# Raw columns for the first group's projections: the reciprocal root applied on the way out of PSUM

## The chip, the cores and the metric

The kernel runs on one core of a Trainium2 chip. Its time is the device time in microseconds of one execution; several executions are timed, and the median is the figure compared. TensorE (PE, with PEld for its weight loads) multiplies matrices into PSUM; VectorE (DVE), ScalarE (ACT) and GpSimd (POOL) work on tiles of 128 partitions; the SyncE queue (SP) issues nearly all transfers, and GpSimd those that add while they write.

## The reference

One layer of a streaming encoder, for 2048 tokens of width 1024, with 16 heads of 64, in float32:

```python
def rms_norm(x, g):
    y = xf * lax.rsqrt(jnp.mean(xf * xf, axis=-1, keepdims=True) + RMS_EPS)
    return (y * g).astype(x.dtype)
...
h = rms_norm(x, g_pre_mix)
m = chunk_relpos_attention(h, w_qkv, w_o, rel_bias)   # 64-token chunks; own chunk and 8 before
x = x + rms_norm(m, g_post_mix)
h = rms_norm(x, g_pre_ffn)
x = x + rms_norm(swiglu(h, w_gate, w_up, w_down), g_post_ffn)
```

The factor of `rms_norm` is one number per token. So the query, key or value of a token can be projected from `x * g` and multiplied by the token's reciprocal root afterwards: both orders give the same result up to rounding.

## The kernel before

Tokens lie in columns: x is held as eight tiles ("columns" k = 0 to 7 in the code) of 128 features by 512 tokens for each half s of a group. There are two groups of 1024 tokens, each with two halves. Every float32 operand is split into a rounded part `hi` and the rest `lo`, and each product is three matmuls (`products`, lines 188 to 190): hi x hi, lo x hi, hi x lo. A query or key block of a head pair p and a half (`qk_job`) is two times eight k-steps of such a triple, 48 matmuls of 512 columns; the values of two head pairs (`v_job`) are 96 matmuls of 256 columns.

TensorE's order is written by hand: a loop over 64 slots per group places scores, transposes and outputs of the attention, and `fill` lets the generator `dense` yield projection matmuls in between, at a rate worked out from when each block is due. All other engines follow an order that a scheduler makes from the program. Small jobs that go with the projections wait in the queue `later`; `tick` takes them from there, one credit for each triple of 512 columns, and `drain` empties it at once. Transposes of scores, the reload of weights and the weight sums for the feed-forward part (`weight_sums`, copies on the SP queue and adding transfers on GpSimd) run alongside.

`begin` is the prologue of group 0. It loads the weights of the first query and key pair (plan[0]) and the eight columns of the first half, splits the columns after multiplying by the gain only (lines 1152 and 1153), and runs query and key projections of the first pair over them, one after the other; the squares are added by GpSimd (line 240). `rstd_steps` sums them over features by matmuls with a vector of ones (`pssq`, line 254), takes the power on GpSimd (line 258) and spreads the root over partitions by four transposes (`prs`, line 270). The first half's queries, keys and values are multiplied by the root when they leave PSUM (lines 1198 and 1203). The second half is loaded into `prep`, squared, and normalised (line 317) and split (lines 340 and 341) before its projections run. Afterwards the first half is loaded once more (`again`), normalised and split, so that all later projections of group 0 read normalised columns. `keep_qk` (lines 474 and 475) splits a query or key block out of PSUM into `stage`, from where transfers put it into `q` and `k`. `said.add(("start", g))` then lets the attention of group 0 begin.

The rows of the relative bias go through a tile `ext` to `ext_d` in memory, at the very start.

Of the kernel before, what the change touches and what calls it, by code (L numbers as in the profile page):

```python
# [47 lines left out]
def trunk(  # L48
# [32 lines left out]
    ones = const.tile([P, P], F32, name="ones")  # L81
# [334 lines left out]

    bias_bufs = []
# [17 lines left out]
    def v_job(g, s, j, w):  # L435
# [6 lines left out]
        for t2 in range(2):  # L442
# [25 lines left out]
    def keep_qk(g, s, p, which, t, scale=None):  # L468
# [3 lines left out]
        scale = (0.125, 1.0)[which] if scale is None else scale  # L472
# [354 lines left out]
    def down_at(c):  # L827
        here = slice(c, min(c + 2, NC))
        return {n: w_d[BLOCK_AT[n]][:, here, :] for n in BLOCK_AT}, {n: sum_d[n][:, here, :] for n in sum_d}

    units = [gate_up_at(c) for c in range(NC)] + [down_at(c) for c in range(0, NC, 2)]
# [299 lines left out]
    def begin(weights):  # L1131

        ap = phase["ap"]
        a, b = heads
        u = Cols(0)
        stage = hb_tile(2, F32, (KT, HALF))
        raw = hb_tile(3, F32, (KT * HALF,))
        for n in range(2):
            ready.append([w_tile(f"{n}_{c}") for c in range(2)])
        second = Prep(1, x[1], PRE_MIX)  # L1140
        second.buffer()
        g_ = gt[:, PRE_MIX, :]
        for k in range(KT):
            if k % 2 == 0:
                s = slice(k * 256, k * 256 + 512)
                sp.dma_start(raw[:, s], plan[0][:, s])
                to = ready[0][k // 4]
                part = slice(k % 4 * 256, k % 4 * 256 + 512)
                split_part(to[0][:, part], to[1][:, part], raw[:, s])
            h = stage[:, k, :]  # L1150
            sp.dma_start(h, x[0][:, k, :])
            act.activation(u.hi(k), h, AF.Copy, scale=g_[:, k : k + 1])
            dve.scalar_tensor_tensor(
                u.lo(k), h, g_[:, k : k + 1], u.hi(k).bitcast(F32), op0=ALU.mult, op1=ALU.subtract
            )
        total = xp.tile([P, HALF], F32, tag="io", name="total_0", bufs=3)
        for k in range(KT):
            add_square(stage[:, k, :], total, k == 0, pool)
        for c in range(2):
            s = slice(c * 1024, c * 1024 + 1024)  # L1160
            part = raw[:, 2048 + c * 1024 : 3072 + c * 1024]
            sp.dma_start(part, plan[1][:, s])
            split_part(*ready[1][c], part)
        for k in range(KT):
            sp.dma_start(second.t[:, k, :], x[1][:, k, :])
        qw = take(ahead=False)
        vw = take(ahead=False)
        rstd = nrm_tile("rstd_0")
        r = const.tile([P, 4], F32, name="rstd_col")
        pts = []  # L1170
        for which in range(2):
            pt = ps.tile([P, HALF], F32, tag="mm", name="pqk")
            c = slice(which * P, which * P + P)
            for k in range(KT):
                products(pt, qw.hi(k, c), qw.lo(k, c), u.hi(k), u.lo(k), k == 0, k == KT - 1)
                yield 3 * C512
            pts.append(pt)
# [3 lines left out]
        def square(k):  # L1181
            return 0.4, lambda: add_square(second.t[:, k, :], second.total, k == 0)

        later.extend(pause(1.5) + rstd_steps(total, rstd, 4.0, keep=r, bank=bank))
        later.extend([square(k) for k in range(KT)] + second.rstd(4.0, bank))
        both = zip(second.norm(), second.split(odd=pool))
        later.extend((0.2, step) for pair in both for _, step in pair)
        v = ap.tile([P, 4, 256], F32, tag="v", name="v_0", bufs=5)
        for t2 in range(2):
            pt = phase["psa"].tile([P, 2, 256], F32, tag="tt", name="pv_", bufs=2)  # L1190
            for n in range(2):
                c = slice((2 * t2 + n) * P, (2 * t2 + n) * P + P)
                for k in range(KT):
                    products(pt[:, n, :], u.hi(k, c), u.lo(k, c), vw.hi(k), vw.lo(k), k == 0, k == KT - 1)
                    yield 3 * C256
            for n in range(2):
                m = 2 * t2 + n
                act.activation(v[:, m, :], pt[:, n, :], AF.Copy, scale=r[:, m : m + 1])
        vs[0, 0, 0] = v
        ts = []  # L1200
        for which in range(2):
            t = xp.tile([P, HALF], F32, tag="io", name="t", bufs=3)
# [292 lines left out]
```

## Time and profile before

| | us |
|---|---|
| median of 3 runs | 2457.96 (2454.76 to 2458.51) |
| the profiled execution | 2454.59 |
| its span, first to last instruction | 2452.8 |
| TensorE busy | 2403.4 (98%) |
| VectorE busy | 1461.6 (60%) |
| ScalarE busy | 1030.7 (42%) |
| GpSimd busy | 295.4 (12%) |

The profile is one execution. Rows of instructions in order of time give the start, the length, engine, line, operation, what is written and read, and in square brackets the idle time ahead and what ended it. A matmul's length overlaps that of the next, so the pace of a run of matmuls is read from start to start. Rows of waits give the total in us, the number of times, and the longest. Rows of stretches give for each engine the busy time and the number of instructions, then the granted TensorE clock, the share of the transfer engines and GB/s. Columns of the second half appear as `prep`, the raw first half as `hb`, blocks on the way out as `stage`.

### The profile page before, as it was taken

The page shows a single profiled execution, that of the slowest core. Times are in us where ns is not written, and L with a number is a line of the kernel's source. Part 1 is how long each engine was busy: PE and PEld are TensorE (multiplying, and loading weights), DVE is VectorE, ACT ScalarE, POOL GpSimd, SP SyncE. Part 2 cuts the span into 40 slices and gives each one's busy share as a digit, 9 for nine tenths or more (in the row PEclk, how much of TensorE's full clock was granted, in tenths as well). Part 3 has the DMA queues.
Part 4 walks back from the last instruction along what each step waited for, and adds up shares of the span by engine and source line. Part 5 has one row for each costly group of instructions (what it writes and reads, how often), then busy time and mean ns, then how long its engine had stood idle before and what let it go on. Part 6 is the DMA issues. An engine that isn't in the chain of part 4 may idle for free.

```text
span 2452.8 us, 34801 instructions
## 1 busy us (share of the span) xinstructions
PE 2403.4 (98%) x12536; PEld 1990.3 (81%) x12536; DVE 1461.6 (60%) x2552; ACT 1030.7 (42%) x1801; POOL 295.4 (12%) x370
## 2 busy tenths in 40 slices
PE   7999999899999999999999999999999999999997
PEld 5887878678888888778888888888888888888886
DVE  6644454567555554558566665677666655555577
ACT  4433444553444443455433333355443333334444
POOL 3122222201222222210000000000000000000001
PEclk9999999999999999999999999999999999999999
DMA  6667897956887867547576755377667665457654
GB/s 186 193 177 194 239 248 199 280 193 207 220 214 199 237 166 196 126 142 238 174 227 212 250 170 188 100 249 252 210 218 256 213 191 154 134 171 244 191 189 149
DMA packets 205276, 490.51 MB, mean 200 GB/s; under 512 B 24848, under 2 KB 26912, under 8 KB 203824
## 3 DMA queue, kind: packets, MB, share of 16 engines
q1 hardware_dynamic: 195312, 453.68, 58.4%
q0 software_dynamic: 9792, 34.61, 8.6%
q8 instruction: 99, 1.62, 0.3%
q14 instruction: 73, 0.60, 0.1%
HBM read 358.64 MB, written 148.42 MB: 207 GB/s over the span
## 4 chain that ended last, share of the span: by engine, by line
PE 54%; DVE 1%; DMA 1%; issue 0%; ACT 0%; DVEq 0%; SPq 0%
PE pd L189 6%; PE pd L188 6%; PE pd L190 6%; PE pb L188 5%; PE pb L189 5%; PE pb L190 5%; PE pa L188 3%; PE pa L189 3%; PE pa L190 3%; PE pc L188 3%; PE pc L190 3%; PE pc L189 3%; PE mm L188 1%; PE mm L190 1%; PE mm L189 1%; DMA y<-y 0%
## 5 line engine op out<-in xcount | busy, mean ns | idle before, releaser
L547 ACT ACTIVATE sc<-sc,nmax 128x640 f32<-128x640 f32 (+4 forms) x256 | 193.1, 756 | 278.4 <-DVE nmax L543 277.8
L188 PE MATMUL mm<-hb,whi 128*128 128x512 f32 x720 | 296.9, 412 | 2.9 <-ACT hb L340 2.4
L189 PE MATMUL mm<-hb,whi 128*128 128x512 f32 x720 | 283.5, 394 | 1.6 <-DVE hb L341 1.0
L190 PE MATMUL mm<-hb,wlo 128*128 128x512 f32 x720 | 283.8, 394 | 0.0
L551 POOL TENSOR_SCALAR sc<-sc,rows 128x640 f32<-128x640 f32 (+4 forms) x256 | 189.6, 742 | 688.1 <-DVE rows L550 652.4
L543 DVE CUSTOM_DVE_ANT_0 sc<-st,bias 128x640 f32<-128x640 f32 (+4 forms) x256 | 179.5, 737 | 104.0 <-PE st L535 101.0
L188 PE MATMUL pb<-hb,whi_gu_T 128*128 128x512 f32 x528 | 206.0, 390 | 3.1 <-DVE terms L955 3.1
L190 PE MATMUL pb<-hb,wlo_gu_T 128*128 128x512 f32 x528 | 205.5, 389 | 0.0
L189 PE MATMUL pb<-hb,whi_gu_T 128*128 128x512 f32 x528 | 205.4, 389 | 0.0
L258 POOL TENSOR_TENSOR rs<-ms,neg_half 128x4 f32<-128x4 f32 (+1 forms) x12 | 17.7, 1479 | 1252.4 <-DVE ms L256 805.7
L188 PEld LDWEIGHTS mm<-hb,whi 128*128 128x128 f32 x720 | 136.1, 189 | 38.4 <-issue 14.6
L190 PEld LDWEIGHTS mm<-hb,wlo 128*128 128x128 f32 x720 | 135.7, 188 | 29.7
L189 PEld LDWEIGHTS mm<-hb,whi 128*128 128x128 f32 x720 | 136.2, 189 | 24.6 <-DVE hb L341 2.5
L188 PE MATMUL mm<-whi,hb 128*128 128x256 f32 x480 | 142.0, 296 | 1.0 <-DVE stage L475 1.0
L189 PE MATMUL pd<-a,whi_d_T 128*128 128x512 f32 (+1 forms) x368 | 140.0, 380 | 0.4 <-DVE a L341 0.4
L188 PE MATMUL pd<-a,whi_d_T 128*128 128x512 f32 (+1 forms) x368 | 140.0, 380 | 0.0
L190 PE MATMUL pd<-a,wlo_d_T 128*128 128x512 f32 (+1 forms) x368 | 139.7, 380 | 0.0
L188 PE MATMUL pa<-hb,whi_gu_B 128*128 128x512 f32 x352 | 137.5, 391 | 0.0
L534 PE MATMUL st<-k,q 128*128 128x384 f32 (+1 forms) x448 | 132.3, 316 | 5.2 <-DVE nmax L543 2.7
L190 PE MATMUL pa<-hb,wlo_gu_B 128*128 128x512 f32 x352 | 137.0, 389 | 0.0
L189 PE MATMUL pa<-hb,whi_gu_B 128*128 128x512 f32 x352 | 136.9, 389 | 0.0
L190 PE MATMUL mm<-whi,hb 128*128 128x256 f32 x480 | 135.6, 282 | 0.0
(222 smaller groups left out, 5563.9 us busy)
## 6 DMA issues: line engine op xcount, KB each, us to landing
raw<-gu_S SPq DMA_DIRECT2D x88, 512.0 KB, 3.8
raw<-in_w_gu SPq DMA_DIRECT2D x66, 512.0 KB, 4.0
q<-stage SPq DMA_DIRECT2D x128, 256.0 KB, 5.4
y<-y SPq DMA_DIRECT2D x96, 256.0 KB, 3.9
gu_S<-in_w_gu SPq DMA_DIRECT2D x44, 512.0 KB, 6.7
raw_a<-aT SPq DMA_DIRECT2D x88, 256.0 KB, 3.6
raw_d<-d_S SPq DMA_DIRECT2D x88, 256.0 KB, 3.6
raw<-in_w_a SPq DMA_DIRECT2D x40, 512.0 KB, 6.1
```

Source lines behind the costliest of these rows:

```text
L188: pe.matmul(pt, a_hi, b_hi, start=first, stop=False, skip_group_check=go_on)
L189: pe.matmul(pt, a_hi, b_lo, start=False, stop=False, skip_group_check=go_on)
L190: pe.matmul(pt, a_lo, b_hi, start=False, stop=last, skip_group_check=go_on)
L258: pool.tensor_tensor(r[0][:, :nb], m[:, :nb], neg_half.to_broadcast([P, nb]), op=ALU.pow)
L534: pe.matmul(st[:, a:b], q[:, 2 * h, cols], kk[:, h, key], start=True, stop=False)
L543: dve.tensor_tensor_reduce(out=sc[:, :n], in0=st[:, c0 : c0 + n], in1=rev, scale=-1.0, scalar=3.0e38, op0=ALU.add, op1=ALU.min, accum_out= ...
L547: act.activation(sc[:, :n], sc[:, :n], AF.Exp, bias=nmax, scale=-1.0, accum_out=rows[:, 0:1])
L551: last_pool[0] = pool.tensor_scalar(sc[:, :n], sc[:, :n], rows[:, 1:2], 1.0, op0=ALU.mult, op1=ALU.mult)
```

## The change

`begin` is rewritten. Both halves are now kept as raw columns times gain, and stay so for all of group 0; there is no second load and no normalisation of columns. Query and key projections take turns within each k-step (`qk`), into two banks. The order on TensorE is: nine matmuls on the identity (`warm`), queries and keys of the first half, its values, queries and keys of the second half (into the scores' banks), its values. The squares of both halves are added by VectorE. `keep_qk` multiplies each query and key block of group 0 by the root into a tile `t` first, and `evacuate_v` copies each 128-token part of the values with the token's root as scale. The bias rows are taken through memory behind the first half's columns (`bias_rows`). The sums of the down weights are made in 11 single units instead of 6 (five double ones and a single one), and the descriptor scratch of GpSimd's transfers is halved.

```diff
-    ones = const.tile([P, P], F32, name="ones")
+    ones = const.tile([P, 1], F32, name="ones")
...
-    with tc.tile_pool(name="extp", bufs=1) as extp:
-        ext = extp.tile([NH, EXT], F32, name="ext")
+    def bias_rows():
+        ext = phase["ap"].tile([P, 6 * HALF], F32, tag="k", name="ext", bufs=2)[0:NH, 0:EXT]
...
-            act.activation(v[:, 2 * t2 : 2 * t2 + 2, :], pt, AF.Copy)
+            if g == 0:
+                evacuate_v(v, t2, pt, s)
+            else:
+                act.activation(v[:, 2 * t2 : 2 * t2 + 2, :], pt, AF.Copy)
...
+    def evacuate_v(v, t2, pt, s):
+        for n in range(2):
+            m = 2 * t2 + n
+            act.activation(v[:, m, :], pt[:, n, :], AF.Copy, scale=rs[s][:, m : m + 1])
...
-    def keep_qk(g, s, p, which, t, scale=None):
+    def keep_qk(g, s, p, which, t):
...
-        scale = (0.125, 1.0)[which] if scale is None else scale
+        scale = (0.125, 1.0)[which]
+        if g == 0:
+            pt, t = t, io("t")
+            dve.scalar_tensor_tensor(t, pt, scale, rows[s], op0=ALU.mult, op1=ALU.mult)
+            scale = 1.0
...
-    units = [gate_up_at(c) for c in range(NC)] + [down_at(c) for c in range(0, NC, 2)]
+    units = [gate_up_at(c) for c in range(NC)] + [down_at(c) for c in range(NC)]
...
+    def begin():
+        ap = phase["ap"]
+        warm = phase["psa"].tile([P, P], F32, tag="po", name="warm", bufs=1)
+        for _ in range(9):
+            pe.matmul(warm, ident, ident, start=True, stop=True)
...
+        def raw(n):
+            return [wp.tile([P, 1024], F32, tag="raw", name=f"raw_{n}_{c}", bufs=2) for c in range(2)]
+        def column(s, k, h):
+            sp.dma_start(h, x[s][:, k, :])
+            act.activation(hts[s].hi(k), h, AF.Copy, scale=g_[:, k : k + 1])
+            dve.scalar_tensor_tensor(
+                hts[s].lo(k), h, g_[:, k : k + 1], hts[s].hi(k).bitcast(F32), op0=ALU.mult, op1=ALU.subtract
+            )
...
+        raws = raw(0)
+        for k in range(KT):
+            if k % 2 == 0:
+                c, here = k // 4, slice(k % 4 * 256, k % 4 * 256 + 512)
+                sp.dma_start(raws[c][:, here], plan[0][:, k * 256 : k * 256 + 512])
+                hi, lo = ready[0][c]
+                split_part(hi[:, here], lo[:, here], raws[c][:, here])
+            column(0, k, cols[0][k])
+        bias_rows()
+        for c, part in enumerate(raw(1)):
+            sp.dma_start(part, plan[1][:, c * 1024 : c * 1024 + 1024])
+            split_part(*ready[1][c], part)
+        for k in range(KT):
+            column(1, k, cols[1][k])
+        for s in range(2):
+            for k in range(KT):
+                add_square(cols[s][k], total[s], k == 0)
...
+        def qk(s, pts):
+            for k in range(KT):
+                for which in range(2):
+                    c = slice(which * P, which * P + P)
+                    products(
+                        pts[which], qw.hi(k, c), qw.lo(k, c), hts[s].hi(k), hts[s].lo(k), k == 0, k == KT - 1
+                    )
+                    yield 3 * C512
+        def norm(s, ahead, wait):
+            steps = rstd_steps(total[s], rows[s], wait, keep=r[s], bank=bank)
+            keep = lambda which: lambda: keep_qk(0, s, 0, which, pts[s][which])
+            later.extend(pause(ahead) + steps + [(0.5, keep(which)) for which in range(2)])
...
+        yield from qk(0, pts[0])
+        norm(0, 14.0, 5.0)
+        later.append((0.5, keep_v))
+        yield from v_products(
+            0, lambda: phase["psa"].tile([P, 2, 256], F32, tag="tt", name="pv", bufs=2)
+        )
+        st = phase["psa"].tile([P, 3 * HALF], F32, tag="S", name="pqk1", bufs=1)
+        pts.append([st[:, n * HALF : n * HALF + HALF] for n in range(2)])
+        rows[1] = const.tile([P, HALF], F32, name="rstd_1")
+        yield from qk(1, pts[1])
+        drain()
+        norm(1, 0.0, 5.0)
+        fetch()
+        yield from v_products(
+            1, lambda: ps.tile([P, HALF], F32, tag="mm", name="pv1").rearrange("p (a b) -> p a b", a=2)
+        )
+        drain()
+        keep_v()
...
-    nc = bacc.Bacc("TRN2", target_bir_lowering=False, num_devices=1, dynamic_dma_scratch_size=1024)
+    nc = bacc.Bacc("TRN2", target_bir_lowering=False, num_devices=1, dynamic_dma_scratch_size=512)
```

The order of transfers on the SP queue at the start, before (`hb3_4` holds raw weights, `hb2_3` the raw first half, `prep` the second half):

```order
L68 DMA gt_81<-in_gains 128x32
L68 DMA hb3_4_180<-in_w_a 128x512
L68 DMA ext_159<-in_rel_bias 16x192
L68 DMA hb2_3_179<-in_x 128x512 x2
L68 DMA hb3_4_180<-in_w_a 128x512
L68 DMA ext_d_155<-ext_159 16x768
L68 DMA hb2_3_179<-in_x 128x512 x2
```

and with the change (`x0_3` is the last pair of first-half columns, `raw_1` the weights of the first values, `x1` the second half):

```order
L68 DMA x0_3_193<-in_x 128x512 x2
L68 DMA ext_236<-in_rel_bias 16x192
L68 DMA raw_1_0_241<-in_w_a 128x1024
L68 DMA raw_1_1_242<-in_w_a 128x1024
L68 DMA x1_194<-in_x 128x512
L68 DMA ext_d_155<-ext_236 16x768
L68 DMA x1_194<-in_x 128x512 x7
```

The two transfers of the bias rows moved from among the first columns to behind all of them, and the second of them now stands ahead of seven columns of the second half.

VectorE between the first half's columns and the second half's projections, before (L317 normalises, L341 splits, `hb_5` and `hb_6` are the second half):

```order
L125 TENSOR_TENSOR wlo_1_188<-hb_4_180,whi_1_187 128x1024
L240 TENSOR_TENSOR prep<-prep,sq 128x512 x6
L256 TENSOR_SCALAR ms<-pssq 128x4
L240 TENSOR_TENSOR prep<-prep,sq 128x512
L1203 SCALAR_TENSOR_TENSOR t<-pqk,rstd_263 128x512 x2
L475 SCALAR_TENSOR_TENSOR stage_0_0_0_499<-t,stage_0_0_0_499 128x512
L475 SCALAR_TENSOR_TENSOR stage_0_0_1_507<-t,stage_0_0_1_507 128x512
L256 TENSOR_SCALAR ms<-pssq 128x4
L317 SCALAR_TENSOR_TENSOR prep<-prep,gt 128x512 x3
L341 TENSOR_TENSOR hb_5_474<-prep,hb_5_474 128x512
```

and with the change (L126 splits weights, L1160 a raw column, L241 adds squares; `hb_4` is the second half, `x_194` the tile with its raw columns and both totals):

```order
L1160 SCALAR_TENSOR_TENSOR hb_2_179<-x_3_193,gt,hb_2_179 128x512 x2
L105 COPY ext<-ext 16x512
L241 TENSOR_TENSOR x_194<-x_194,sq 128x512 x2
L126 TENSOR_TENSOR wlo_0_187<-raw_0_241,whi_0_186 128x1024
...
L1160 SCALAR_TENSOR_TENSOR hb_4_185<-x_194,gt,hb_4_185 128x512
L241 TENSOR_TENSOR x_194<-x_194,sq 128x512 x7
L257 TENSOR_SCALAR ms<-pssq 128x4
L486 SCALAR_TENSOR_TENSOR t<-pqk,rstd_195 128x512 x2
L490 SCALAR_TENSOR_TENSOR stage_0_0_0_502<-t,stage_0_0_0_502 128x512
```

The copy that the bias rows wait for and two additions stand ahead of the value weights, and the second half's additions ahead of the first half's mean (L257).

VectorE in group 0's attention, at the first pair's keys and queries after the prologue, before:

```order
L475 SCALAR_TENSOR_TENSOR stage_0_1_0_822<-mm,stage_0_1_0_822 128x512
L543 ISA sc,nmax<-st,bias_746 128x384
L543 ISA nmax 128x1
L543 ISA sc,nmax<-st,bias_751 128x384
...
L550 RECIPROCAL rows<-rows 128x1 x2
```

and with the change:

```order
L486 SCALAR_TENSOR_TENSOR t<-mm,rstd_195 128x512
L490 SCALAR_TENSOR_TENSOR stage_0_1_0_798<-t,stage_0_1_0_798 128x512
L558 ISA sc,nmax<-st,bias_720 128x384
L558 ISA nmax 128x1
L558 ISA sc,nmax<-st,bias_725 128x384
...
L565 RECIPROCAL rows<-rows 128x1 x2
```

Each block takes one instruction more, with a tile in between. On TensorE the sequence of matmuls behind the prologue is the one it was.

More of the change, by code (lines that the diff above doesn't have):

```diff
@@ L415, in trunk @@
     qs, ks, vs, bias = {}, {}, {}, {}
+    rows, rs = {}, []
     bias_bufs = []
@@ L1169, in begin @@
[L1169 to L1173, printed above, removed]
+            column(1, k, cols[1][k])
+        for s in range(2):
             for k in range(KT):
-                products(pt, qw.hi(k, c), qw.lo(k, c), u.hi(k), u.lo(k), k == 0, k == KT - 1)
-                yield 3 * C512
-            pts.append(pt)
+                add_square(cols[s][k], total[s], k == 0)
@@ L1178, in bank @@
+        qw, vw = take(ahead=False), take(ahead=False)
         def bank(name):
             return phase["psa"].tile([P, 4, P], F32, tag="po", name=name, bufs=1)
[L1181 to L1187, printed above, removed]
@@ L1199, in begin @@
[L1199 to L1202, printed above, removed]
-            dve.scalar_tensor_tensor(t, pts[which], (0.125, 1.0)[which], rstd, op0=ALU.mult, op1=ALU.mult)
-            ts.append(t)
-        drain()
-        for which in range(2):
-            keep_qk(0, 0, 0, which, ts[which], 1.0)
-        weights.extend((qw, vw))
-        again = Prep(0, x[0], PRE_MIX)
-        again.r = rstd
-        later.extend(again.load_only() + again.norm() + again.split())
+        def qk(s, pts):
[6 more added lines that the diff above has]
+                    yield 3 * C512
@@ L1221, in dense @@
                     if g == 0:
-                        weights = []
-                        yield from begin(weights)
-                        qw, vw = weights
+                        yield from begin()
+                        said.add(("start", g))
+                        continue
                     else:
```

81 lines of the change are left out of this document (32 added, 49 removed).

## The prediction

> **What bounds the kernel now.** I read the whole page first, then busy time by stretch, then TensorE's waits and its instructions in order of time for the stretch that the change rewrites, and last VectorE, GpSimd and the SyncE queue there. By stretch (columns: stretch, length, then busy time and instructions of PE, PEld, DVE, ACT, POOL; granted clock, DMA share, GB/s):
>
> ```profile
> span 2452.8 us, 34801 instructions
> 0.00:20.00 20.00, 10.66 (x19) 5.38 (x19) 12.82 (x15) 14.78 (x24) 9.85 (x20) 1.00 0.85 280
> ...
> 76.58:436.00 359.42, 358.51 (x2273) 301.35 (x2271) 178.11 (x481) 149.80 (x341) 95.72 (x138) 1.00 0.77 206
> ```
>
> From 76.58 us on TensorE is busy for 358.51 of 359.42 us: group 0's attention starts when the prologue lets it, and then TensorE alone sets the pace. So a microsecond won before 76.58 should be a microsecond of the span, and a microsecond of VectorE work added behind it should cost nothing (VectorE idles half of that time). The prologue itself, in TensorE's order:
>
> ```profile
> 6.32 0.79 PE L188 MATMUL pqk<-hb,whi 128*128 128x512 f32 x1 [6.32 <-ACT hb L1152]
> ...
> 23.38 0.63 PE L188 MATMUL pqk<-hb,whi 128*128 128x512 f32 x1
> 25.94 0.53 PE L188 MATMUL pqk<-hb,whi 128*128 128x512 f32 x1
> 28.16 0.39 PE L188 MATMUL pqk<-hb,whi 128*128 128x512 f32 x1
> 29.98 0.39 PE L190 MATMUL pqk<-hb,wlo 128*128 128x512 f32 x1
> 32.00 0.95 PE L254 MATMUL pssq<-ones,total 128*128 128x1 f32 x8
> 32.81 0.36 PE L188 MATMUL pv__316<-whi,hb 128*128 128x256 f32 x1
> 36.49 0.60 PE L270 MATMUL prs<-ident,rstd_col 128*128 128x128 f32 x4
> 36.84 0.36 PE L188 MATMUL pv__316<-whi,hb 128*128 128x256 f32 x1
> 41.04 0.28 PE L188 MATMUL pv__382<-whi,hb 128*128 128x256 f32 x1
> 43.80 0.28 PE L190 MATMUL pv__382<-whi,hb 128*128 128x256 f32 x1
> 46.94 0.80 PE L188 MATMUL mm<-hb,whi 128*128 128x512 f32 x1 [2.43 <-ACT hb L340]
> 48.21 0.80 PE L189 MATMUL mm<-hb,whi 128*128 128x512 f32 x1 [0.47 <-DVE hb L341]
> 53.31 0.49 PE L188 MATMUL mm<-hb,whi 128*128 128x512 f32 x1
> 76.58 0.40 PE L188 MATMUL mm<-hb,whi 128*128 128x512 f32 x1
> ```
>
> Start to start, six 512-column matmuls from 23.38 to 25.94 take 0.427 us each, eight from 28.16 to 29.98 take 0.2275: two clocks. The 256-column ones take 0.12 (23 steps from 41.04 to 43.80). The prologue's work at the fast clock is 2 x 48 x 0.2275 + 2 x 96 x 0.12 = 44.9 us, plus for each half 0.81 (32.00 to 32.81) and 0.35 (36.49 to 36.84) for the norm's small matmuls: 47.2 us. From 6.32 that would end at 53.5; it ends at 76.58. **23.1 us** are lost, in three places: waits for the first columns and the slow clock until 26; the wait for the normalised second half at 44 to 48; the slow clock again until 53.31. The waits, in us:
>
> ```profile
> PE pqk L188 <- ACT hb L1152: 7.7, 2, 6.3
> PE pqk L189 <- DVE hb L1153: 3.2, 3, 1.7
> PE mm L188 <- ACT hb L340: 2.4, 1, 2.4
> ```
>
> **The change part by part: the first half.** Queries and keys of the first half now use each column as it lands, six matmuls instead of three, so work is there to keep TensorE busy while columns come. The columns' own limit was VectorE (order of time; then one line's instructions, ns shortest, median, longest; groups: busy us, mean ns):
>
> ```profile
> 19.05 3.45 DVE L1153 SCALAR_TENSOR_TENSOR hb<-hb,gt,hb 128x512 fp32r<-128x512 f32 x2
> ...
> L1153 DVE SCALAR_TENSOR_TENSOR hb<-hb,gt,hb x8: 736/1042/1769, 6.3 to 20.7; 128x512 fp32r<-128x512 f32 x8
> L1153 DVE SCALAR_TENSOR_TENSOR hb<-hb,gt,hb 128x512 fp32r<-128x512 f32 x8 | 9.5, 1202 | 4.0 <-ACT hb L1152 4.0
> L125 DVE TENSOR_TENSOR wlo<-hb,whi 128x512 fp32r<-128x512 f32 x4 | 4.9, 1228 | 0.0
> L240 DVE TENSOR_TENSOR prep<-prep,sq 128x512 f32<-128x512 f32 x7 | 4.8, 691 | 0.5
> L240 POOL TENSOR_TENSOR total<-total,sq x7: 1262/1359/1619, 8.9 to 20.3; 128x512 f32<-128x512 f32 x7
> ```
>
> L1153 takes 736 ns at its shortest and up to 1769 while GpSimd adds the squares, from 8.9 to about 22. Those adds move to VectorE, most of them behind the columns. At the shortest L1153, and for L125 at the 0.69 that a subtraction or addition of this shape takes in L240's row, the columns save 8 x (1.20 - 0.74) + 4 x (1.23 - 0.69) = 5.8 us.
>
> SyncE also no longer stops for the bias rows ahead of the columns:
>
> ```profile
> 1.84 0.34 SPq L68 DMA_DIRECT2D ext<-in_rel_bias  x1
> 3.17 0.43 SPq L68 DMA_DIRECT2D hb<-in_w_a  x1
> 4.51 0.33 SPq L68 DMA_DIRECT2D ext_d<-ext  x1
> ```
>
> That gives 0.4 us before the first column and 0.9 more before the third (from 3.60 to 4.51). So the last column's low part, which ended at 22.5, should end near 22.5 - 5.8 - 1.3 = 15.4. First matmul 6.32 - 0.4 = 5.9. At the fast clock 48 matmuls (10.9 us) end at 16.8 at the earliest, with small gaps 17.5. If the clock stays slow as long as from 46.94 to 53.31 (6.4 us), it costs 6.4 x (1 - 0.2275/0.427) = 3.0 us. The nine identity matmuls have no row. Nine transposes at L270's 0.35 for four would last 0.8 us, nine of the first matmul's 0.79 last 7.1. I take nine at the slow 0.43 pace, 3.9 us, nearest to a cold start. They wait for the identity:
>
> ```profile
> 1.01 0.29 POOL masks.py:199 TENSOR_SCALAR_AFFINE_SELECT ident<-ident 128x128 f32<-128x128 f32 x1
> ```
>
> ready at 1.30, now some 0.4 later behind two bias corners. So they end at 5.6, before the first column; at 7.1 us they delay it by 2.9. Range for the end of the first 48: 16.8 to 21.
>
> The Trainium skill, "TensorE: Matmul & The Clock Gate", section "Part 1: The HAM clock gate", says that about 3.4 us of sustained work releases the clock and an idle window of about that length takes it back. By it the identity matmuls warm TensorE in time and the 48 end at 16.8; the trace is less kind, since 2.43 and 0.47 us of idleness were followed by 6.4 slow us.
>
> **First values.** Their weights are split behind the columns. VectorE does the ext copy (0.4), two adds (1.4) and the first half's 1.2 after 15.4, so TensorE starts at 18.4; the second half is ready 1.9 later and the fifth k-step needs it 1.4 after the start: 0.5 wait. 18.4 + 0.5 + 11.5 + 0.8 = **31.2**.
>
> **Second half.** The norm, its splitting, the reload of x and the repeated norm and split go away; with them the waits at 44 to 48 and the slow clock behind. New in SyncE's way: the second value weights wait for a raw buffer that VectorE frees, and seven columns stand behind the ext_d write, which waits for a copy that VectorE reaches only at about 15.8. Before, the eight loads took
>
> ```profile
> 11.51 7.45 SPq L68 DMA_DIRECT2D prep<-in_x  x8
> 33.23 1.42 POOL L258 TENSOR_TENSOR rstd_col<-ms,neg_half 128x4 f32<-128x4 f32 x1 [11.28 <-DVE ms L256]
> ```
>
> 0.93 us each; so the last leaves at 23 and, given the prologue's rate of 280 GB/s, lands near 25; needed from 31.2 on, so hidden, and the cover is 6 us. VectorE then adds the second half's squares (7 x 0.69) ahead of the first half's mean, at 30.5, with TensorE's sums at about 30; power 1.42, so the reciprocal root stands at 32.3, and its spreading is due 3.5 us after 31.2. If that is 2 us late, TensorE waits 0. Second 48: 31.2 + 10.9 + 0.35 = 42.5. Second values with both small pieces: 42.5 + 11.5 + 1.2 = **55.2**, against 76.58: 21.4 us won; 16 to 23 with the ends above.
>
> **Group 0 behind it.** TensorE's order is the same from here. Each query and key block takes one multiplication more on VectorE, 28 of them (seven pairs, two halves, query and key), and 28 x 0.69 (L475's mean below) = 19 us fit into its idle 181. What counts is lateness: TensorE waited once for a key block in group 0, at
>
> ```profile
> 436.32 0.33 PE L534 MATMUL st<-k,q 128*128 128x128 f32 x1 [1.23 <-DMA k<-stage]
> L475 DVE SCALAR_TENSOR_TENSOR stage<-mm,stage 128x512 fp32r<-128x512 f32 x26 | 17.9, 689 | 25.6 <-ACT stage L474 22.7 <-DMA bias<-ext_d 2.3 <-DMA gu_S<-in_w_gu 0.5
> 240.00:260.00 20.00, 20.00 (x113) 17.46 (x112) 9.68 (x26) 9.39 (x21) 5.65 (x8) 1.00 1.03 286
> ```
>
> There the extra step adds its 0.69 and one queue position, together 1.3 us (0.7 to 3). Other pairs have more time, since the rate is set by the last pair. Weight sums: 22 units instead of 17, so 96 steps over the 120 slots instead of 76. Group 0 takes about 11 steps more, each a copy and an add; the last ones being halved, that is some 8 MB on top of 206 GB/s x 359 us = 74. The stretch 240 to 260 had 286 GB/s and no wait, so I charge 0.5 us (0 to 4). Splitting value evacuations in two stays on ScalarE, idle for 210 us of this stretch.
>
> **Sum.** 21.4 - 1.3 - 0.5 = 19.6 won. The profiled execution took 2454.59 (span 2452.8): 2435.0. The median 2457.96 lies 3.4 above that: 2438.4 by it. I forecast **2437**, own range 2431 to 2443.
>
> **The rivals.** (a) *The prologue wins only half*: late columns delay the squares, the sums' matmuls wait 3 us, and two slow-clock spells cost 3.0 each: 21.4 - 9 - 1.8 = 10.6, about 2446. For it: the slow clock came twice. Against: six matmuls a column keep TensorE busier than arrivals. (b) *Group 0 hands it back*: a wait like that at 436.32 at each of the 14 block starts behind the first pair, 0.7 each, about 10 us, 2447. For it: DMA share near 1 in places; against: one such wait in 360 us. The Trainium skill, "SBUF — State Buffer", section "Who interferes with whom", says that a VectorE instruction with two SBUF inputs and a GpSimd one that reads SBUF shut each other out. The rows of L1153 beside the adds agree. By it the new subtraction, whose inputs both lie in SBUF, could meet a multiplication of GpSimd (1.61 for two, below) and the block at 436.32 would come up to 0.8 us later still: 18.8 won instead of 19.6, 2438. (c) *GpSimd is held by its sum transfers*, because the software queue's scratch is halved, which makes the kernel slower:
>
> ```profile
> 259.25 0.82 POOL L843 DMA_DIRECT2D gu_S<-in_w_gu  x1
> 263.13 1.61 POOL L551 TENSOR_SCALAR sc<-sc,rows 128x640 f32<-128x640 f32 x2 [3.06 <-DVE rows L550]
> 269.50 1.04 PE L567 MATMUL tt<-ident,sc 128*128 128x128 f32 x8
> DMA to landing us min/median/max: 4.1/7.9/10.5
> ```
>
> An issue takes 0.82; then GpSimd has 3.06 spare, and its result (at 264.74) is read 4.76 later. So a hold up to 8.6 us is free; at 9.2, midway between median and longest landing, 88 issues (four adds for each of 22 units) lose 0.6 each, 53 us: 2490. Against: the largest transfers are halved with it. (d) *Nothing*: something later pins the end; 2456. Against: the first fence.
>
> **Chances.** Forecast 0.72, (a) 0.14, (b) 0.06, (c) 0.03, (d) 0.05. Range 2428 to 2449: it holds the forecast's own range and (a) and (b). A change under 0.2% (5 us) cannot be told from none: faster 0.92, same 0.05, slower 0.03.
>
> **What would show it.** Right: the prologue's last matmul at about 55 instead of 76.58, no TensorE wait over 1 us between the first column and there, 0.23 us per 512-column matmul from about 10 us on, squares without L1153 above 0.8 us, and group 0 as long as before within 3 us. Wrong: waits for the sums' matmuls near 30 or for hb at 31 (a); several waits for k in group 0 (b); GpSimd DMA instructions of several us, with transposes behind them (c).

## The result, and the profile after

| | before | after |
|---|---|---|
| median | 2458.51 us (2454.03 to 2462.48, 19 runs) | 2444.97 us (2438.08 to 2456.54, 19 runs) |
| the profiled execution | 2454.59 us, span 2452.8 | 2441.23 us, span 2439.5 |

The ratio is 0.9947, with a 95% interval of 0.9937 to 0.9957: the change makes the kernel 13.5 us faster by the medians. The forecast was 2437, so it is 8 us slower than forecast. That is outside the forecast's own range of 2431 to 2443, and inside the wide range of 2428 to 2449, which was drawn to hold two rivals too.

**The prologue** went nearly as worked out. TensorE in order of time, kernel after (start, length, engine, line, operation, what it writes and reads, idle time ahead):

```profile
1.63 4.00 PE L1151 MATMUL warm<-ident 128*128 128x128 f32 x18 [1.63 <-POOL ident masks.py:199]
6.12 0.49 PE L189 MATMUL pqk<-hb,whi 128*128 128x512 f32 x1 [0.49 <-ACT hb L1159]
...
17.95 0.39 PE L191 MATMUL pqk<-hb,wlo 128*128 128x512 f32 x1
18.18 0.28 PE L189 MATMUL pv<-whi,hb 128*128 128x256 f32 x1
18.88 0.39 PE L190 MATMUL pv<-wlo,hb 128*128 128x256 f32 x1 [0.43 <-DVE wlo L126]
29.95 0.95 PE L255 MATMUL pssq<-ones,x 128*128 128x1 f32 x8
31.55 0.40 PE L189 MATMUL pqk<-hb,whi 128*128 128x512 f32 x1
34.98 0.60 PE L271 MATMUL prs<-ident,rstd_col 128*128 128x128 f32 x4
42.93 0.28 PE L189 MATMUL pv<-whi,hb 128*128 128x256 f32 x1
55.63 0.28 PE L191 MATMUL pv<-whi,hb 128*128 128x256 f32 x1
55.75 0.40 PE L189 MATMUL mm<-hb,whi 128*128 128x512 f32 x1
56.45 0.22 PE L549 MATMUL st<-k,q 128*128 128x128 f32 x1
```

The nine identity matmuls stand as 18 instructions and end at 5.63. The 47 steps from 6.12 to 17.95 take 11.83 us, 0.25 each, so the pace is fast from the first column on. The reader finds three stage starts to set against the forecast: 31.55, 42.93 and the last prologue matmul at 55.63. The group of VectorE's column splits, from 0 to 30 us (busy us, mean ns, then idle time):

```profile
L1160 DVE SCALAR_TENSOR_TENSOR hb<-x,gt,hb 128x512 fp32r<-128x512 f32 x16 | 11.3, 748 | 1.8 <-ACT hb L1159 1.7
```

748 ns in the mean and none above 755, against a mean of 1202 before, when GpSimd added the squares beside it.

**Group 0** gave a large part back. I cut each trace at three places: the first score matmul (`st`), the first matmul of the sixteenth output block of the attention (`po`, the end of group 0's attention) and that of the thirty-second (the end of group 1's). The rest is mostly the feed-forward part. Two profiles of the kernel before and three of the change were taken; e5, e9 and e10 are runs told of below.

| us | first score | to the end of group 0 | to the end of group 1 | rest | span |
|---|---|---|---|---|---|
| before | 77.28 | 420.9 | 594.7 | 1359.9 | 2452.8 |
| before, e9 | 77.33 | 420.1 | 598.8 | 1361.1 | 2457.3 |
| after | 56.45 | 429.0 | 592.7 | 1361.4 | 2439.5 |
| after, e5 | 56.56 | 431.4 | 591.5 | 1369.4 | 2448.9 |
| after, e10 | 56.45 | 432.0 | 595.8 | 1361.3 | 2445.5 |

By the means of these rows the prologue wins 20.8, group 0 loses 10.3 (430.8 against 420.5), group 1 wins 3.4 and the rest loses 3.5, all of it in e5: 10.4 us won in all. The medians won 13.5, 11.0 and 10.7 in the three sets of runs that hold the change itself.

The loss sits late in group 0's attention. TensorE's longest waits in its second half, in order of time, kernel after:

```profile
366.18 1.42 PE L582 MATMUL tt<-ident,sc 128*128 128x128 f32 x8 [0.67 <-POOL sc L566]
417.05 0.44 PE L593 MATMUL tt<-ident,sc 128*128 128x128 f32 x2 [1.53 <-ACT pT L587]
419.16 0.45 PE L549 MATMUL st<-k,q 128*128 128x128 f32 x1 [1.67 <-DMA k<-stage]
451.69 0.41 PE L549 MATMUL st<-k,q 128*128 128x384 f32 x1 [1.73 <-DVE nmax L558]
457.51 2.37 PE L611 MATMUL po<-pT,v 128*64 128x512 f32 x14 [3.40 <-ACT pT L587]
466.22 0.80 PE L189 MATMUL mm<-hb,whi 128*128 128x512 f32 x1 [3.52 <-ACT y L236]
```

Together 12.5 us, 11.9 of them from 416 us on. The kernel before has waits there too. The two of them above 0.5 us for the key block are at 436.32 and 437.56 (1.23 and 0.81), and the two longest that follow are:

```profile
469.05 0.41 PE L534 MATMUL st<-k,q 128*128 128x384 f32 x1 [2.66 <-DVE nmax L543]
471.86 4.53 PE L596 MATMUL po<-pT,v 128*64 128x512 f32 x16 [1.07 <-DVE pT L570]
```

All of its waits above 0.5 us in group 0 come to 7.4 us, against 12.5 in the change. The stretch from 360 to 420 us behind the first score, in the view of stretches (length, busy time of PE, PEld, DVE, ACT, POOL, granted clock, DMA share, GB/s), first before, then after:

```profile
437.28:497.28 60.00, 53.88 (x285) 40.64 (x285) 35.37 (x83) 32.27 (x66) 14.98 (x21) 0.94 0.97 295
```

```profile
416.45:476.45 60.00, 48.76 (x243) 37.27 (x244) 33.69 (x81) 29.85 (x63) 16.34 (x22) 0.91 1.01 285
```

TensorE places 42 fewer matmuls in it, and the share of the transfer engines rises from 0.97 to 1.01. ScalarE shows what is late. Its instructions in order of time, and then the SyncE queue's (the attention's columns `al` are loaded back there for the output projection):

```profile
448.05 1.28 ACT L341 ACTIVATE hb<-al 128x512 fp32r<-128x512 f32 x2 [3.37 <-DMA al<-attn]
...
455.76 1.21 ACT L341 ACTIVATE hb<-al 128x512 fp32r<-128x512 f32 x2 [1.85 <-DMA al<-attn]
456.88 0.58 ACT L587 ACTIVATE pT<-tt 128x512 f32<-128x512 f32 x1
```

```profile
445.11 5.29 SPq L68 DMA_DIRECT2D al<-attn  x3
450.46 1.81 SPq L68 DMA_DIRECT2D d_S<-in_w_d  x3
457.15 0.33 SPq L68 DMA_DIRECT2D al<-attn  x1
```

In ScalarE's order the copy `pT` at 456.88, for which TensorE waits until 457.51, stands behind two splits of `al` that waited for their transfers. These two columns were issued at 445.11 and 449.44, ahead of the three copies of weight sums (`d_S`), and landed 10.6 and 6.9 us later. The fourteen `al` loads between 340 and 420 us behind the first score take 6.0 us to land in the median, against 5.0 in the kernel before. ScalarE's waits for them over the whole of group 0 (total, times, longest), after and before:

```profile
ACT hb L341 <- DMA al<-attn: 15.2, 9, 3.5
```

```profile
ACT hb L340 <- DMA al<-attn: 11.4, 8, 3.8
```

So ScalarE waited for these columns before as well. TensorE's waits behind ScalarE in group 0 were 0.92 and 0.48 us then and are 1.53, 3.40 and 3.52 now. The rows show the chain; they do not show why 3.8 us more of ScalarE's waits cost TensorE that much more.

### The profile page after: what moved, and what is told of

Its sections match the earlier page's. It is cut to its first block, busy times and chain, and to the rows that moved or that the text cites. A ratio compares the mean times of both kernels' runs of the same rounds, so it can differ in the third digit from the quotient of the medians.

```text
span 2439.5 us, 34920 instructions
## 1 busy us (share of the span) xinstructions
PE 2400.2 (98%) x12554; PEld 1994.3 (82%) x12554; DVE 1466.2 (60%) x2569; ACT 1033.1 (42%) x1807; POOL 299.2 (12%) x379
## 4 chain that ended last, share of the span: by engine, by line
PE 52%; DMA 2%; DVE 2%; issue 0%; ACT 0%; SPq 0%; DVEq 0%; ACTq 0%
PE pd L190 6%; PE pd L189 6%; PE pd L191 6%; PE pb L189 4%; PE pb L191 4%; PE pb L190 4%; PE pa L189 3%; PE pa L191 3%; PE pa L190 3%; PE pc L189 3%; PE pc L190 3%; PE pc L191 3%; PE mm L189 1%; PE mm L191 1%; PE mm L190 1%; DMA y<-y 1%
## 5 line engine op out<-in xcount | busy, mean ns | idle before, releaser
L189 PE MATMUL mm<-hb,whi 128*128 128x512 f32 x704 | 290.7, 413 | 3.5 <-ACT y L236 3.5
L191 PE MATMUL mm<-hb,wlo 128*128 128x512 f32 x704 | 277.6, 394 | 0.0
L190 PE MATMUL mm<-hb,whi 128*128 128x512 f32 x704 | 276.5, 393 | 0.0
L189 PEld LDWEIGHTS mm<-hb,whi 128*128 128x128 f32 x704 | 133.1, 189 | 38.1 <-issue 14.7
L190 PEld LDWEIGHTS mm<-hb,whi 128*128 128x128 f32 x704 | 133.5, 190 | 19.5
L189 PE MATMUL mm<-whi,hb 128*128 128x256 f32 x448 | 132.8, 296 | 0.0
L126 DVE TENSOR_TENSOR wlo_gu_T<-raw,whi_gu_T 128x1024 fp32r<-128x1024 f32 x88 | 107.5, 1221 | 42.1 <-ACT whi_gu_T L125 41.7
```

The source lines that it names most:

```text
L126: dve.tensor_tensor(lo, raw, hi.bitcast(F32), op=ALU.subtract)
L189: pe.matmul(pt, a_hi, b_hi, start=first, stop=False, skip_group_check=go_on)
L190: pe.matmul(pt, a_hi, b_lo, start=False, stop=False, skip_group_check=go_on)
L191: pe.matmul(pt, a_lo, b_hi, start=False, stop=last, skip_group_check=go_on)
```

## The experiments

The first question was why group 0 takes longer. There were four candidates in the change: more steps of weight sums over the attention (96 in place of 76), the halved scratch of GpSimd's transfers, the tile `t` that takes a buffer from the ring of small tiles, and the extra multiplication itself.

**e1: the tile in another place.** The product goes into the block's own stage.

```diff
+        stage = ap.tile([P, 2, HALF], F32R, tag="stage", name=f"stage_{g}_{s}_{p}_{which}", bufs=2)
...
-            pt, t = t, io("t")
+            pt, t = t, stage[:, 1, :].bitcast(F32)
...
-        stage = ap.tile([P, 2, HALF], F32R, tag="stage", name=f"stage_{g}_{s}_{p}_{which}", bufs=2)
```

> The change, but the multiplied block t is written into the second half of stage and split there in place, so it takes none of the three io buffers that the attention outputs and their reloads (al) turn over. From the first score to the last output of group 0 the kernel before takes 420.9 us, the change 429.0. If the io buffers are what delays al at the end of group 0 (theory IO), that stretch comes back to 421 to 423 and the time is about 6 us below the change (ratio to before 0.992). If the extra VectorE step, the halved descriptor scratch or the faster weight sums cost it, the stretch stays at 427 to 430 and the ratio at 0.9947.

Median 2443.3 (2442.87 to 2444.29), ratio 0.9932 (0.9921 to 0.9944); first score 56.27, then 429.5 to the end of group 0. By the stretch, the buffer is not it. The ratio lies between the two expected and decides nothing, and the same holds for e2 and e4.

**e2: the scratch as before.**

```diff
-        rows[1] = const.tile([P, HALF], F32, name="rstd_1")
+        rows[1] = rows[0]
...
-dynamic_dma_scratch_size=512
+dynamic_dma_scratch_size=1024
```

> The change with the descriptor scratch of before (1024 instead of 512). To make room the two halves share one tile for the spread root, so from the second pair on the first half's queries and keys are multiplied by the second half's root: the work is the same, that factor is not. Theory SCRATCH: GpSimd's stops ahead of its sum transfers (112.8 us over 30 in the change, none before) vanish, the stretch from first score to last output of group 0 falls from 429.0 to 421 to 424, and the ratio to before from 0.9947 to about 0.992. The theories IO, RATE (more weight-sum transfers in group 0) and STEP (the extra VectorE step) expect the stops to vanish without effect: 427 to 430, 0.9947.

Median 2444.59 (2442.25 to 2448.54), ratio 0.9939 (0.9926 to 0.9952); group 0 takes 428.1. GpSimd's idle time ahead of its adding transfers, us in all, times, longest, in the change and then here:

```profile
POOL gu_S L857 <- issue: 106.3, 28, 7.3
```

```profile
POOL gu_S L857 <- issue: 3.0, 1, 3.0
```

So the halved scratch does hold GpSimd, up to 7.3 us at a time in this profile, and most of it is hidden: with the stops gone group 0 is 0.9 us shorter than in the first profile of the change. TensorE waits elsewhere instead:

```profile
420.69 0.69 PE L593 MATMUL tt<-ident,sc 128*128 128x128 f32 x2 [5.83 <-ACT pT L587]
...
458.44 2.04 PE L611 MATMUL po<-pT,v 128*64 128x512 f32 x7 [3.36 <-ACT pT L587]
```

**e3: the sums of group 0 at their old pace.** Nothing is left out; the steps saved in group 0 are taken in group 1.

```diff
-                if m > 4 and (m * n_sums) // 120 > ((m - 1) * n_sums) // 120:
+                due_by = lambda m: m * 76 // 120 if m <= 64 else 40 + (m - 64) * 56 // 56
+                if m > 4 and due_by(m) > due_by(m - 1):
```

> The change, but group 0 takes weight-sum steps at the pace of before (76 in 120 slots) and group 1 takes the rest, one a slot. Theory RATE: the stretch from first score to last output of group 0 falls from 429.0 to 421 to 424, group 1 takes 0 to 3 us more, ratio about 0.993. SCRATCH expects part of that, since spacing shortens GpSimd's stops (112.8 us to about 60): 425, 0.994. IO and STEP expect 427 to 430 and 0.9947.

Median 2441.97 (2439.99 to 2446.24), ratio 0.9927 (0.9914 to 0.9940). Group 0 takes 420.9, to the tenth what it took before. The last 60 us again:

```profile
416.95:476.95 60.00, 53.70 (x285) 41.49 (x285) 36.50 (x86) 33.58 (x67) 16.65 (x22) 0.97 0.99 301
```

285 matmuls as before, with the extra multiplications, the small scratch and the ring of the change all in place. The run differs from the change in the pace of the sums alone, so that pace makes the loss. The median shows less of it than the 8 us, since the rest took 1367.3 in this profile: a wait of 2.77 us at 1374 in the feed-forward part, and the slow clock behind it.

**e4: without the extra multiplication** of the query and key blocks of pairs 1 to 7.

```diff
-        if g == 0:
+        if g == 0 and p == 0:
```

> The change without the multiplication by the root for queries and keys of pairs 2 to 8 in group 0 (that factor is left out), so the blocks go from PSUM to stage as before. It takes away the extra VectorE step and its io buffer. Theories STEP and IO: the stretch from first score to last output of group 0 falls from 429.0 to 421 to 423, ratio about 0.992. SCRATCH and RATE: it stays at 427 to 430, ratio 0.9947; the single wait for a key block (1.67) falls by about 1.3.

Median 2446.98 (2439.97 to 2449.97), ratio 0.9941 (0.9925 to 0.9956); group 0 takes 427.5, 1.5 us below the shortest of the change's three and 3.3 below their mean. The three differ by 3.0 among themselves, so one profile cannot price the step. The wait for the key block fell from 1.67 to 0.20 us as expected, but TensorE waited 2.11 us for `pT` just ahead of it. In e3, with all the multiplications in place, group 0 takes what it took before, so nothing shows that the step costs time.

**e5: the change once more**, as a mark.

> The change itself, unaltered, as the mark for the three runs beside it. If the theory that group 0 gives back about 8 us is right, the first score starts near 56.4, and from there to the last output of group 0 it takes 427 to 430 us; the median lies 13 to 17 us below the kernel before. Rival, that the loss in group 0 was an accident of one profile: the stretch takes about 421 here.

Median 2449.07 (2446.13 to 2457.56), before 2460.06, ratio 0.9960 (0.9946 to 0.9975); 431.4 in group 0. The rest took 1369.4, with waits of 2.29 and 3.51 us for `terms`. The loss in group 0 was no accident of one profile.

**e6: the sums alone**, on the kernel before.

```diff
...
-    units = [gate_up_at(c) for c in range(NC)] + [down_at(c) for c in range(0, NC, 2)]
+    units = [gate_up_at(c) for c in range(NC)] + [down_at(c) for c in range(NC)]
...
-dynamic_dma_scratch_size=1024
+dynamic_dma_scratch_size=512
```

> The kernel before with nothing changed but the weight sums: the down weights in 11 single units, so 96 steps over the attention in place of 76, and the transfers' scratch on GpSimd halved; its prologue is the old one. Theory RATE (the faster pace of the sums costs group 0 about 8 us, whatever the prologue is): first score at 77 as before, the stretch from there to group 0's last output 427 to 430 instead of 420.9, median 4 to 9 us above the kernel before (ratio 1.002 to 1.004). Rival PROLOGUE (the sums hurt only because the new prologue leaves raw columns and one more multiplication behind): stretch 421, ratio 1.000.

Group 0 takes 432.2, 11 to 12 us more than the kernel before, with the old prologue and normalised columns: the cost in group 0 belongs to the sums, whatever stands ahead. The median moved less than expected, 2462.0 against 2460.06, ratio 1.001 (1.000 to 1.002). In the profile the first score came at 72.15 instead of 77.3, and group 1 took 591.1 instead of 594.7 and 598.8, which hides most of the loss in the total. In that prologue the column splits on VectorE and the adds on GpSimd met in another order in time, and the columns were ready at 19.2 us instead of 21.8 to 22.5. Why they did is open.

**e7: the down weights' sums later.** 52 steps over the attention, 44 behind it.

```diff
-                if m > 4 and (m * n_sums) // 120 > ((m - 1) * n_sums) // 120:
+                if m > 4 and (m * 52) // 120 > ((m - 1) * 52) // 120:
...
-    for _ in sums:
-        pass
-    for c in work:
+    for n, c in enumerate(work):
         tick(c / (3 * C512))
+        if n % 11 == 0:
+            next(sums, None)
```

> The change with its 96 steps of weight sums kept, but paced otherwise: 52 over the 120 slots of the attention (enough for the gate and up weights, which are read first), the other 44 for the down weights one by one within the rest of the attention's tail and the gate and up products. Theory RATE: group 0 carries fewer transfers than in the kernel before, so the stretch to group 0's last output is 421 or shorter, down to 413 if the waits that the kernel before had there go too; the feed-forward part, whose transfers are busy 0.5 to 0.75 of the time, takes no more than 3 us longer. Median 2430 to 2440, and below the change by 6 to 14. Rival: the load moves to the feed-forward part and costs there what it saved, median as the change's.

Median 2463.45 (2457.96 to 2469.82), ratio 1.0014 (1.0005 to 1.0024): slower than the kernel before. Group 0 takes 420.6, the top of the expected figures, but the rest 1382.9. Two of TensorE's waits there, and GpSimd at the second:

```profile
1158.00 0.80 PE L189 MATMUL pa<-hb,whi_gu_B 128*128 128x512 f32 x1 [6.13 <-ACT terms L950]
1235.94 0.65 PE L271 MATMUL prs<-ident,rs 128*128 128x128 f32 x4 [4.21 <-POOL rs L259]
```

```profile
1227.00 0.84 POOL L857 DMA_DIRECT2D d_S<-in_w_d  x1 [4.31 <-issue]
1233.57 0.82 POOL L857 DMA_DIRECT2D d_S<-in_w_d  x1 [5.73 <-issue]
1234.12 1.77 POOL L259 TENSOR_TENSOR rs<-ms,neg_half 128x4 f32<-128x4 f32 x1
```

Here the stop ahead of an adding transfer is paid in full: the power for a norm stands behind it, and TensorE waits 4.21 us for it. The rival of this run was right, and cost more than it said.

**e8: one identity matmul** instead of nine.

```diff
-        for _ in range(9):
+        for _ in range(1):
```

> The change with one matmul on the identity at its start in place of nine. Theory CLOCK (the nine keep TensorE busy long enough to have the fast clock from the first column on): the 512-column matmuls start 0.43 us apart instead of 0.23 up to about 12 us, and the first score comes 1.5 to 3 us later than 56.4. Rival COLUMNS (the first 48 matmuls wait for columns anyway until about 15 us): the first score comes less than 0.7 us later.

```profile
1.63 0.80 PE L1151 MATMUL warm<-ident 128*128 128x128 f32 x2 [1.63 <-POOL ident masks.py:199]
6.41 0.79 PE L189 MATMUL pqk<-hb,whi 128*128 128x512 f32 x1 [3.98 <-ACT hb L1159]
...
11.63 0.60 PE L191 MATMUL pqk<-hb,wlo 128*128 128x512 f32 x1
12.05 0.40 PE L189 MATMUL pqk<-hb,whi 128*128 128x512 f32 x1
...
31.06 0.95 PE L255 MATMUL pssq<-ones,x 128*128 128x1 f32 x8
```

Twelve matmuls run at the slow pace, until 12.05. The view's clock column reads 1.00 over these 5.64 us, as it does over the slow start of the kernel before, so at the start the pace shows only in the starts of the matmuls. The sums' matmuls come at 31.06 instead of 29.95 and the first score at 57.56: 1.1 us later in this one profile, between the two theories' figures. The slow stretch was there as the one said; a part of it cost nothing, because of the columns, as the other said.

**e9: the kernel before, once more.**

> The kernel before, unaltered, for a second profile of it. In the run with the sums alone the same old prologue reached the first score at 72.15 where the profile before had 77.28. Theory LUCK (the old prologue's end hangs on how the clock falls, and the profile before was one of its long ones): first score between 71 and 76 here, so part of the 20.8 us read from two profiles was never there in the medians. Rival: 77 again, and the 72.15 came with the edit. The stretch to group 0's last output should be 418 to 424 in both cases; at 428 or more the loss of group 0 would be chance too.

First score 77.33, group 0 420.1, 2459.1 us. The theory that the old prologue was long by luck falls; the 72.15 of e6 stays without a cause.

**e10, e11, e12: the change, the old pace, and early sums**, side by side. In e12 all 96 steps stay in the attention, but none lies in slots 45 to 62:

```diff
-                if m > 4 and (m * n_sums) // 120 > ((m - 1) * n_sums) // 120:
+                due_by = lambda m: min(m - 4, 16) + max(0, min(m, 44) - 20) * 2 // 3 + max(0, m - 62) * 64 // 58
+                for _ in range(due_by(m) - due_by(m - 1) if m > 4 else 0):
```

> The change, unaltered, as the mark for the two kernels beside it: first score 56 to 57, stretch to group 0's last output 427 to 432, median 2440 to 2449.

> The change with the weight sums of group 0 at their old pace (76 steps per 120 slots up to slot 64, then one step a slot), timed beside the change on one chip. Theory RATE: stretch 420 to 423 and the median 3 to 8 us below the change. Rival (what group 0 gains the feed-forward part loses by a wait and a slow clock, as it did in the single profile of the first such run): median within 1.5 us of the change.

> The change with the same 96 steps of sums in the attention, but early: one a slot in slots 5 to 20, two in three slots up to 44, none from 44 to 62 (where the change waits for query and key blocks and for attention columns), the rest from there on. Theory RATE, put more sharply (only the transfers in slots 44 to 62 hurt): stretch 417 to 422, median 3 to 10 us below the change. Rival (the burst in the first slots costs as much there, at least one wait over 2 us for sc or k in slots 5 to 20): stretch 425 or more.

| | median (range, runs) | ratio to before (2459.47) | group 0 | group 1 | rest |
|---|---|---|---|---|---|
| e10, the change | 2448.80 (2439.77 to 2451.32, 7) | 0.9952 (0.9935 to 0.9969) | 432.0 | 595.8 | 1361.3 |
| e11, old pace | 2441.40 (2437.71 to 2445.60, 6) | 0.9927 (0.9911 to 0.9944) | 422.3 | 594.5 | 1365.3 |
| e12, early | 2440.16 (2435.54 to 2444.78, 6) | 0.9924 (0.9906 to 0.9943) | 415.0 | 599.7 | 1366.0 |

Both repaced kernels have medians 7 to 9 us below the change, and e12's group 0 is 5 to 6 us shorter than that of the kernel before, below the 417 to 422 expected. The last two stretches of 60 us of it, and ScalarE's waits for the attention columns (15.2 us in the change):

```profile
356.59:416.59 60.00, 60.00 (x421) 52.48 (x419) 29.39 (x81) 25.94 (x62) 13.41 (x20) 1.00 0.49 137
416.59:476.59 60.00, 57.28 (x321) 43.15 (x320) 40.20 (x90) 34.07 (x70) 11.89 (x17) 1.00 0.80 259
```

```profile
ACT hb L341 <- DMA al<-attn: 2.0, 3, 0.8
```

The transfer engines are busy 0.80 of the time instead of 1.01, the columns come in time, TensorE places 321 matmuls instead of 243, and the clock stays at 1.00. Ahead of these two stretches TensorE's only waits above 0.5 us are 0.95 and 0.73 (at 206.68 and 239.24), well under what was freed. By slot 44 the change and e12 have both taken 32 steps of sums; from there to slot 62 the change takes 14 more and e12 none. So leaving these slots free is enough to take the loss away. It does not show that the loss comes from these slots alone: e3 takes 12 steps in them and 25 ahead of them, and has no loss either. The late transfers cost time together with the fuller load ahead of them, and no run separates the two. In e12 the 14 steps fall to group 1, which takes 599.7 against 594.5 in e11 and 593.3 in the mean of the change's three: about 5 us of what group 0 won over e11 is lost again there. e12 is the fastest kernel of this study by its median; e11's range overlaps it, and one cannot be told from the other.

## Why the prediction was right in its range and 8 us off

**The prologue: right.** First matmul 5.9 forecast, 6.12 measured; end of the identity matmuls 5.6 and 5.63; first 48 ended 17.5 and 18.18; second half's queries 31.2 and 31.55; second values 42.5 and 42.93; end 55.2 and 55.75. TensorE never waited over 0.5 us between the first column and there. The first score came 20.8 us earlier against a term of 21.4. VectorE's split came down to 748 ns as taken from its shortest row. One reading was too short: the three places named for the 23.1 us lost account for about 19 of them by the starts of the matmuls, and the rest lies in small waits behind 53.31.

**The clock: right, but cheaper.** It was costed at 3.0 us if the slow spell came; e8, where it came, was 1.1 us later in its one profile. The Trainium skill, "TensorE: Matmul & The Clock Gate", section "Part 1: The HAM clock gate", puts the release after about 3.4 us of sustained work. In the change 4.00 us of identity matmuls were followed by the fast pace at once, which agrees; in e8 it took 5.64 us from the first column (6.41 to 12.05), which is longer.

**The key block at 436.32: not the place.** I charged 1.3 us for the extra step. I wrote that the kernel before waited once for a key block; it waits twice, at 436.32 and again 0.81 us at 437.56. The change waits for the key block 1.8 us in one profile, 2.8 in e5 and not at all in e10, where a wait of 5.29 us for `pT` stands at that place, so this term can be neither confirmed nor refused.

**The weight sums: the step that failed.** The forecast said: "The stretch 240 to 260 had 286 GB/s and no wait, so I charge 0.5 us (0 to 4)." The 8 MB were right: 4 copies and 9 adds of 512 KB more and 6 copies of 256 KB stand in group 0. Their price was 8.1, 10.5 and 11.1 us in three profiles, and it goes, to within 2 us, when they are taken at the old pace (420.9 in e3, 422.3 in e11). A stretch that carries 286 GB/s without a wait says that nobody in it was waiting for a late transfer. It says nothing of slots 48 to 64, where the loads of attention columns, weights of the output projection and the last key blocks have their due times, and where the kernel before already had a DMA share of 0.97. I had the view of stretches and read one of them for all. The first fence, from which I took that TensorE alone sets the pace, ends at 436.00, and every wait above 0.5 us of the kernel before in group 0 stands behind it, the first at 436.32. The test of the prediction, group 0 as long as before within 3 us, failed by it. That the median still lies inside the range of 2428 to 2449 is in part luck: the range reached that far for (a) and (b), and neither happened as described.

**The rivals.** (b) had the size, about 10 us handed back by group 0 and 2447, and the wrong mechanism: the waits are not one for `k` at each block's start but a few of 1.5 to 5 us at the end, mostly behind ScalarE. (c) had a real mechanism: GpSimd stopped up to 7.3, 10.1 and 7.4 us ahead of adding transfers in the change's three profiles. TensorE's longest wait for GpSimd's `sc` was 0.67, 2.64 and 2.93 us in them, so most of the stops fell into spare time, as the prediction's 8.6 us of slack said, but not all. (a) and (d) did not occur. That group 1 got 3.4 us shorter was not forecast; in both profiles of before a wait of 2.9 to 3.1 us for `pT` near 686 stands there and not in the change. The wait comes back, at 1.8 to 3.1 us, in e3, e7, e11 and e12, which take fewer sums in group 0, and in none of the runs that take them at the pace of the change. So it goes with the sums; by what path was not tested.

## What to carry to other kernels

Price background transfers in the stretch with the tightest due times, not by the average and not by a full stretch that happened to have no wait: look for the slots in which other work waits for transfers, and try keeping the background out of these. Keeping them out of those slots altogether freed 6 us more of group 0 than thinning them over the whole group (e12 against e3), but group 1 lost about as much (599.7 against 593.1), so price the stretch that receives them too. Moving them behind the attention cost more than they had cost in the first place (e7). When a change has two parts, run each alone: here one won 21 us ahead of the first score and the other, carried along, lost 8 to 11 in group 0; in the medians, which hold the rest of the kernel too, the slower pace won 7 us back (e11 against e10).

## What was not expected of the hardware

With half the scratch, GpSimd stood up to 10.1 us ahead of an adding transfer (94.6 to 106.3 us in all over the first group in three profiles, 3.0 with the full scratch), and these stops are idle time that no row of an instruction shows: they stand as "issue" ahead of the next one. In e7, where the adding transfers follow each other, the two quoted start 6.57 us apart.

A wait can cost more than its length. The granted clock of the change's profile (`after`) falls to half in two spells in group 0:

```profile
418.29:425.12 6.83, 5.79 (x19) 4.98 (x20) 3.92 (x13) 2.83 (x8) 2.34 (x4) 0.50 1.06 276
466.08:469.49 3.41, 3.27 (x9) 2.58 (x10) 1.85 (x3) 2.01 (x4) 0.58 (x1) 0.50 1.01 382
```

The first begins within the second of two waits of 1.53 and 1.67 us that follow each other, the second at the end of the wait of 3.52 us. Not every wait does this: after those of 1.73 and 3.40 us, between the two spells, the clock stays at 1.00. At half pace the 9.06 us of busy time in them cost about 4.5 us, as an estimate. e12 has no such spell in group 0.

The clock explains only a part of the scatter between executions. Of 46 executions of the kernel before, timed beside the experiments, those with a mean clock of 0.994 took 2459.4 us in the mean and those with 0.992 took 2462.4, but those with 0.993 lie anywhere from 2456.33 to 2465.24. A gain read from two single profiles can be several us off.
